# A hybrid encoder layer on one core: column weights stored as whole blocks of 128 columns

## The chip, the core and the metric

The kernel runs on one core of a Trainium2 chip. The metric is the time of one execution on the device, in microseconds. The kernel before takes 1960.93 us (median of 3 runs, 1960.2 to 1962.21). One more execution was taken with the hardware profiler on; it took 1962.87 us, of which 1961.1 us are the span between its first and its last instruction. All statements on waits and engines come from that execution.

The engines are TensorE (PE, matrix products; PEld is its loading of the stationary operand), VectorE (DVE), ScalarE (ACT), GpSimd (POOL) and SyncE (SP). In this kernel SP computes nothing; it issues transfers, and so does POOL. Transfers that SP issues are queue 1 of the profile, those that POOL issues are queue 0. The data of both are moved by the same 16 DMA engines.

## What is computed

The layer works on 1024 tokens of width 1024, in float32. With `rms` a root-mean-square norm with a learnt gain:

```python
h = x + 0.5 * (silu(n1 @ w_gate1) * (n1 @ w_up1)) @ w_down1       # n1 = rms(x), d_ff = 2816
z = rms(h) @ w_in                                                 # 1024 x 4352, cut into qA kA vA qB kB vB gA gB
yA = neighbourhood attention on a 16 x 64 grid, 8 heads, learnt relative bias
yB = banded attention, 8 query and 2 key/value heads, rope, one sink logit a head
h = h + (sigmoid(gA) * (yA @ w_a) + sigmoid(gB) * (yB @ w_b)) @ w_out
h = h + 0.5 * (silu(n2 @ w_gate2) * (n2 @ w_up2)) @ w_down2       # n2 = rms(h)
y = rms(h)
```

Seven of the weights stand on the left of a product in the kernel, so that it needs them a block of columns at a time: `w_gate` and `w_up` of both feed-forward parts (1024 x 2816 each), `w_in` (1024 x 4352) and the two branch weights `w_a` and `w_b` (512 x 1024 each). The change is to these seven. `w_down` and `w_out` are not touched.

## The kernel before

**Precision.** Each factor is split into a high part and a remainder (`split`, lines 86 to 89): ACT rounds the source to the short format (line 88), DVE, or POOL in a few places, subtracts that from the source (line 89). A product then takes three matmuls (`mm3`, lines 137 to 144): high by high (line 140), high by remainder (142), remainder by high (144). So before PE can start on a weight block, the block must have landed, ACT must have cast it and DVE must have subtracted.

**Fewer products.** The feed-forward parts, the larger part of the input projection and the output projection multiply 2 x 2 blocks with seven products in place of eight (`products`, line 241; its mirror for `w_down` and `w_out` is the class `Down`). For one step `i` and one of two matrices or column groups `m`, two blocks of 128 columns are loaded, each as 1024 rows by 128 columns: `raws[i, m, 0]` and `raws[i, m, 1]`. `prep(q)` (line 279) adds and subtracts quarters of them on DVE, splits the result, and `multiply(q)` (line 305) runs 4 x 3 matmuls of 128 x 512 on it. `prep` runs up to eight entries ahead of `multiply` (line 338 onwards). After every product `after` copies or adds the bank on ACT or DVE; the next product into the same bank waits for that.

**Loads of the seven weights.** Five places issue them, all on SP:

- `fetch` (line 277), called by `load` in `prep` for the raw blocks, and by `load_ahead` for the first entries of step 1;
- `load_ahead` (line 274), halves of blocks of step 2 (the first four of the eight groups of 128 rows for P1, the other four for P2);
- `load_split` (line 95), called by `load_w` for the blocks of `w_in` that make the gates gA and gB, which fill PE's time during attention (`gate`, line 890);
- `fetch_branch` (line 905), blocks of `w_a` and `w_b`, of 512 rows.

All take their source from `w_cols`:

```python
def w_cols(w, c0, n=P):
    return w[:, c0:c0 + n].rearrange("(c p) f -> p c f", p=P)
```

The weight lies in device memory row by row. A block of 128 columns is therefore 1024 pieces (512 for a branch weight) of 128 floats, 512 bytes, and partition p of the tile receives eight (four) of them: rows p, p + 128, p + 256 and so on.

**Buffers.** A raw tile is 128 x 1024 floats, 512 KB. There are four of them (tag `raw`), and `products` borrows two more from `fx` or `fa`. A new block can be requested only when the last reader of the old one is done, so SP waits in `fetch` for DVE.

**Stages in order of time.** First norm and transposes (0 to about 40 us); the first feed-forward part's gate and up (to about 430); its down projection (to about 610); a turn, in which the finished rows are normed, transposed and split while the first products of the next stage begin (`transition`, line 159; to about 690); the input projection (to about 860), with `rope` (line 701), which writes z to device memory, reads it back rotated and writes it again; attention with the gates as filler (to about 1146); branch products, merge and output projection (to about 1300); a second turn (to about 1380); the second feed-forward part (to the end).

**What sets the order.** The program text gives a priority; the framework's planner then writes out one fixed instruction list for each engine at build time, with its own estimates of how long each instruction and each transfer takes, and puts in the waits. On the chip each engine runs its list in order. In the profile of before one sees that the list isn't the order of the text: the casts for `T3` and `T4` (`strassen_rest`, line 225) stand on ACT ahead of the norm of the last row tile, which the text has earlier.

Of the kernel before, what the change touches and what calls it, by code (L numbers as in the profile page):

```python
# [15 lines left out]
P = 128  # L16
# [20 lines left out]
def trunk_kernel(ctx, tc, x, n1, wg1, wu1, wd1, nm, win, rpb, sink, wa, wb, wo,  # L37
# [12 lines left out]
    def nm_(s):  # L50
        uid[0] += 1
        return f"{s}_{uid[0]}"
# [25 lines left out]
    def raw4():  # L78
        return main.tile([P, 1024], F32, tag="raw", bufs=4, name=nm_("raw"))
# [4 lines left out]
    def ws4():  # L84
        return main.tile([P, 1024], F32R, tag="ws", bufs=8, name=nm_("ws"))

    def split(dst_hi, dst_lo, src, eng=None):
        nc.scalar.copy(dst_hi, src)  # L88
        (eng or nc.vector).tensor_tensor(dst_lo, src, f32v(dst_hi), op=ALU.subtract)  # L89

    def load_split(h, l, src_ap, a, b, r=None, eng=None):

        n = a * b
        r = raw4() if r is None else r
        nc.sync.dma_start(r[:, :n].rearrange("p (a b) -> p a b", a=a), src_ap)
        split(h[:, :n], l[:, :n], r[:, :n], eng)
        return (h[:, :n].rearrange("p (a b) -> p a b", a=a), l[:, :n].rearrange("p (a b) -> p a b", a=a))

    def w_cols(w, c0, n=P):
        return w[:, c0:c0 + n].rearrange("(c p) f -> p c f", p=P)  # L100

    def load_w(w, c0, r=None, eng=None):

        return load_split(ws4(), ws4(), w_cols(w, c0), w.shape[0] // P, P, r, eng)

    def load_gain(g):
        gb = const.tile([P, 1152], F32, tag="gain", bufs=1, name=nm_("gain"))
# [259 lines left out]
    def hidden(wg, wu, at_end):  # L367
# [4 lines left out]
        def after(i, p, m, bks, snap, sn):  # L372
# [37 lines left out]
            else:  # L410
# [14 lines left out]
                else:  # L425
# [5 lines left out]
                    put(i, "P6", s2)  # L431

        return products(lambda i, m, half: w_cols((wg, wu)[m], (i + half * NP) * P), NP, after, at_end, (6, 7),
                        [8, 9, 10, 11, 0, 1, 2, 3, 4, 5, 6, 7])

# [351 lines left out]
    def gate_first():  # L787
        mix["gate"] = load_w(win[0], GA + gates[0] * P, xs4())
# [10 lines left out]
    for c in range(4):  # L799
# [7 lines left out]
    hook(2, gate_first)  # L807
    hook(0, keep_u)
    pg = products(lambda i, m, half: w_cols(win[0], groups[i][m][half] * P), NG, store_z, at_end, (2, 3), range(8, 16),
                  ("P1", "P2", "P5", "P6", "P7", "P3", "P4"))  # L810
    down.into(transition(down1, gain, to_strassen, behind(pg), 2), pg)
# [144 lines left out]
    def filler():  # L956
        for dc, nxt in zip(gates, gates[1:] + [None]):
            if nxt is not None:
                yield from gate(dc, lambda: mix.update(gate=load_w(win[0], GA + nxt * P)))
            else:  # L960
                yield from gate(dc, lambda: [load_y(Y_B[c], c * P, nc.gpsimd) for c in range(2)])
        yield from branch_b()
        for i in range(2):
            branch_a(i)
            for _ in range(3):
                drain(a_mm[i][1], 1)
                yield
# [126 lines left out]
    for n in range(1 << 30):  # L1094
# [14 lines left out]
        if n in (59, 60, 61):  # L1109
            c = (59, 60, 61).index(n)  # L1110
# [53 lines left out]
    for i, dc in enumerate(a_order):  # L1164
        r = nxt.pop(0)
# [49 lines left out]
def _consts():  # L1215
# [14 lines left out]
    for cols in ((left, full, right), (full, full, full)):  # L1230
# [7 lines left out]
    return {"c_rope": rope, "c_mask_a": mask_a, "c_mask_b": mask_b}  # L1238


_INS = ['x', 'ffn1_norm', 'ffn1_w_gate', 'ffn1_w_up', 'ffn1_w_down', 'mix_norm', 'w_in', 'na_rpb', 'sink_logit',
        'w_branch_a', 'w_branch_b', 'w_out', 'ffn2_norm', 'ffn2_w_gate', 'ffn2_w_up', 'ffn2_w_down', 'final_norm']
_OUTS = [((1, 1024, 1024), 'float32')]
# [21 lines left out]
```

## Time and profile before

| | |
|---|---|
| median of 3 runs | 1960.93 us |
| profiled execution | 1962.87 us, span 1961.1 us |
| PE busy | 1927.7 us, 98% of the span |
| DVE / ACT / POOL busy | 1442.4 / 951.7 / 335.7 us |
| granted clock of PE, mean | 0.998 |
| bytes moved | 293.46 MB in 263554 packets |
| SP's queue | 206912 packets, 206.24 MB, 34.1% of the DMA engines' time |
| POOL's queue | 56512 packets, 85.58 MB, 15.3% |

The lines below are of these kinds. The page's first part gives an engine, its busy time and its instructions. The timeline gives start, duration (both us), engine, line of the code, operation, the tile written and the tiles read, shape, number, and in brackets the idle time of that engine just before it with what ended it. The view of stretches gives for a stretch of time the busy time of each engine with the number of instructions, PE's granted clock (1.00 is full), the busy share of the 16 DMA engines and the rate at which they moved data. On SP's timeline a row is the issue of a transfer, not its course.

### The profile page before, as it was taken

The numbers are of one execution on the slowest core, as the hardware profiler recorded it, in microseconds if no ns is written. First come the engines' busy times: TensorE is split into PE (matmuls) and PEld (weight loads), VectorE is DVE, ScalarE is ACT, GpSimd is POOL, SyncE is SP. The second block draws the span as 40 slices with busy tenths as digits, with TensorE's granted clock in tenths as the row PEclk, the third lists the DMA queues.
The fourth block names the chain that finished last, engine by engine and source line by source line (L and its number), as shares of the span: only waits on it lengthen the run. The fifth ranks groups of instructions, "written<-read, shape, count | busy, mean of one in ns | idle before, by whom it ended". The sixth has DMA issues, their size and how long they took to land. (4 is left out here: it accounts for less than half of the span.)

```text
span 1961.1 us, 25643 instructions
## 1 busy us (share of the span) xinstructions
PE 1927.7 (98%) x8968; PEld 1605.7 (82%) x8968; DVE 1442.4 (74%) x2543; ACT 951.7 (49%) x1845; POOL 335.7 (17%) x429
## 2 busy tenths in 40 slices
PE   7999999999999999999999999999999999999998
PEld 5888888888888878888888888887888888888886
DVE  7885566558967778678888857999766567559864
ACT  7433333334446543467787873366333333344452
POOL 1010011003400022311112135500101001005200
PEclk9999999999999999999999999999999999999999
DMA  6533323367243489953359565543433333493341
GB/s 195 172 119 123 102 92 120 110 221 268 85 125 122 136 206 241 227 177 92 101 137 195 179 223 209 178 145 98 150 108 113 108 97 102 142 347 107 116 137 60
DMA packets 263554, 293.46 MB, mean 150 GB/s; under 512 B 47072, under 2 KB 193888, under 8 KB 263424
## 3 DMA queue, kind: packets, MB, share of 16 engines
q1 hardware_dynamic: 206912, 206.24, 34.1%
q0 software_dynamic: 56512, 85.58, 15.3%
q8 instruction: 71, 1.16, 0.3%
q14 instruction: 59, 0.48, 0.1%
HBM read 205.16 MB, written 86.70 MB: 149 GB/s over the span
## 5 line engine op out<-in xcount | busy, mean ns | idle before, releaser
L140 PE MATMUL g<-ar,ws 128*128 128x512 f32 x1184 | 444.7, 397 | 8.0 <-ACT xs L901 1.9
L142 PE MATMUL g<-ar,ws 128*128 128x512 f32 x1184 | 437.5, 391 | 0.6 <-DVE ar L89 0.6
L144 PE MATMUL g<-ar,ws 128*128 128x512 f32 x1184 | 435.7, 390 | 1.5 <-DVE ws L89 1.5
L89 DVE TENSOR_TENSOR ws<-raw,ws 128x512 fp32r<-128x512 f32 (+1 forms) x329 | 239.4, 733 | 180.7 <-ACT ws L88 179.4
L88 ACT CAST ws<-raw 128x512 fp32r<-128x512 f32 (+1 forms) x331 | 209.1, 638 | 289.3 <-PE d L144 129.6
L144 PEld LDWEIGHTS g<-ar,ws 128*128 128x128 f32 x1184 | 222.7, 188 | 49.0 <-DVE ws L89 1.9
L140 PE MATMUL d<-ar,ws 128*128 128x512 f32 x680 | 262.3, 390 | 0.0
L142 PE MATMUL d<-ar,ws 128*128 128x512 f32 x680 | 261.9, 389 | 0.0
L144 PE MATMUL d<-ar,ws 128*128 128x512 f32 x680 | 261.9, 389 | 0.0
L142 PEld LDWEIGHTS g<-ar,ws 128*128 128x128 f32 x1184 | 223.0, 188 | 47.4 <-DVE ar L89 1.1
L140 PEld LDWEIGHTS g<-ar,ws 128*128 128x128 f32 x1184 | 217.5, 189 | 51.0 <-ACT ar L88 4.2
L140 PEld LDWEIGHTS d<-ar,ws 128*128 128x128 f32 x680 | 127.7, 188 | 26.5
L144 PEld LDWEIGHTS d<-ar,ws 128*128 128x128 f32 x680 | 127.6, 188 | 26.4
L142 PEld LDWEIGHTS d<-ar,ws 128*128 128x128 f32 x680 | 127.7, 188 | 26.3
L370 POOL DMA_DIRECT2D hid<-fx x96 | 51.8, 540 | 402.1 <-DVE fx L418 168.9
L89 DVE TENSOR_TENSOR ws<-ar,ws 128x512 fp32r<-128x512 f32 x114 | 108.1, 956 | 9.0 <-ACT ws L88 9.0
L88 ACT CAST ar<-raw 128x512 fp32r<-128x512 f32 (+1 forms) x83 | 56.0, 678 | 88.3 <-PE g L142 47.9
L89 DVE TENSOR_TENSOR ws<-fa,ws 128x512 fp32r<-128x512 f32 x76 | 52.5, 691 | 57.7 <-ACT ws L88 57.4
L140 PE MATMUL g<-ws,ws 128*128 128x512 f32 x232 | 91.0, 392 | 0.0
L142 PE MATMUL g<-ws,ws 128*128 128x512 f32 x232 | 90.4, 390 | 0.0
L144 PE MATMUL g<-ws,ws 128*128 128x512 f32 x232 | 90.3, 389 | 0.0
L1042 ACT ACTIVATE fa<-fa,nmx 128x385 f32<-128x385 f32 (+3 forms) x128 | 75.5, 591 | 26.2 <-DVE nmx L1039 25.5
(237 smaller groups left out, 3516.6 us busy)
## 6 DMA issues: line engine op xcount, KB each, us to landing
raw<-hid SPq DMA_DIRECT2D x70, 512.0 KB
hid<-fx POOLq DMA_DIRECT2D x96, 256.0 KB, 2.3
raw<-in_ffn_w_up_dram SPq DMA_DIRECT2D x32, 512.0 KB
ar<-in_ffn_w_down_dram SPq DMA_DIRECT2D x32, 512.0 KB
raw<-in_ffn_w_gate_dram SPq DMA_DIRECT2D x28, 512.0 KB
hid<-fa POOLq DMA_DIRECT2D x54, 256.0 KB, 2.3
raw<-in_w_in_dram SPq DMA_DIRECT2D x27, 512.0 KB
ar<-zs_d POOLq DMA_DIRECT2D x48, 256.0 KB, 5.0
```

The lines of the kernel that those rows point to most:

```text
L88: nc.scalar.copy(dst_hi, src)
L89: (eng or nc.vector).tensor_tensor(dst_lo, src, f32v(dst_hi), op=ALU.subtract)
L140: nc.tensor.matmul(b, lhs[0], r[0], start=first, stop=False, **kw)
L142: nc.tensor.matmul(b, lhs[0], r[1], start=False, stop=False, **kw)
L144: nc.tensor.matmul(b, lhs[1], r[0], start=False, stop=last, **kw)
L370: nc.gpsimd.dma_start(hid[PRODUCTS.index(p), i], src)
L1042: nc.scalar.activation(pr, pr, AF.Exp, scale=-1.0, bias=nmx[:, s:s + 1], accum_out=ssum[:, s:s + 1])
```

## The change

The host reorders each of the seven weights before the run: it cuts the matrix into blocks of 128 columns, and inside a block stores for each of the 128 partitions all the values that this partition will receive, one after the other. A block then is one stretch of 512 KB (256 KB for a branch weight), in which partition p's 4 KB (2 KB) are contiguous. `w_cols` picks a block by its number and gives it the old shape, (p, c, f). The tiles receive the same values in the same places. `load_w` takes the number of rows from the last dimension, since the first no longer holds it. The number of loads, their bytes, their destinations and their issuers stay.

```diff
-    def w_cols(w, c0, n=P):
-        return w[:, c0:c0 + n].rearrange("(c p) f -> p c f", p=P)
+    def w_cols(w, c0):
+        return w[c0 // P].rearrange("p (c f) -> p c f", f=P)
 
     def load_w(w, c0, r=None, eng=None):
 
-        return load_split(ws4(), ws4(), w_cols(w, c0), w.shape[0] // P, P, r, eng)
+        return load_split(ws4(), ws4(), w_cols(w, c0), w.shape[-1] // P, P, r, eng)
...
+def _blocks(w):
+
+    k, n = w.shape[1:]
+    return w.reshape(k // P, P, n // P, P).transpose(2, 1, 0, 3).reshape(1, n // P, P, k)
+
+
+_BLOCKED = ['ffn1_w_gate', 'ffn1_w_up', 'w_in', 'w_branch_a', 'w_branch_b', 'ffn2_w_gate', 'ffn2_w_up']
...
-    data = {name: inputs[name] for name in _INS}
+    data = {name: _blocks(inputs[name]) if name in _BLOCKED else inputs[name] for name in _INS}
```

The reordering is done on the host ahead of the launch and is not part of the time.

## The prediction

> **What bounds the kernel now.** I read the page's first part, then the stretches, then every idle time of PE.
>
> ```profile
> span 1961.1 us, 25643 instructions
> PE 1927.7 (98%) x8968; PEld 1605.7 (82%) x8968; DVE 1442.4 (74%) x2543; ACT 951.7 (49%) x1845; POOL 335.7 (17%) x429
> DMA packets 263554, 293.46 MB, mean 150 GB/s; under 512 B 47072, under 2 KB 193888, under 8 KB 263424
> q1 hardware_dynamic: 206912, 206.24, 34.1%
> ```
> ```profile
> 200.00:220.00 20.00, 20.00 (x90) 16.55 (x89) 15.87 (x25) 7.68 (x13) 2.16 (x4) 1.00 0.23 79
> 1340.00:1360.00 20.00, 20.00 (x90) 16.57 (x89) 19.80 (x34) 8.85 (x17) 0.54 (x1) 1.00 0.36 104
> ```
>
> PE is busy for 1927.7 of 1961.1 us. In a steady stretch (200 to 220) it starts some 89 matmuls in 20 us, 0.225 us each, at full clock, while the DMA engines are busy 0.23 of the time. A load that lands sooner there shortens nothing: SP waits for room and PE waits for nobody.
>
> ```profile
> SPq L277 <- DVE ws L89: 599.3, 89, 24.0
> ```
>
> In the list of SP's waits that is the largest: 599.3 us, in 89 waits, until DVE gives a raw buffer back. So the change can only act through the 33.4 us in which PE is idle, and only where the last thing that PE's chain waits for is one of the seven weights.
>
> The largest part of that idle time is the start, and there it isn't:
>
> ```profile
> 10.57 1.06 ACT L118 ACTIVATE xs<-fx 128x1024 f32<-128x1024 f32 x1 [0.16 <-DMA fx<-in_x_dram]
> 20.26 0.79 PE L140 MATMUL g<-ar,ws 128*128 128x512 f32 x1 [0.57 <-ACT ar L88]
> 29.78 0.50 PE L144 MATMUL g<-ar,ws 128*128 128x512 f32 x1 [1.48 <-DVE ws L89]
> 20.00:40.00 20.00, 17.80 (x81) 14.23 (x82) 19.22 (x31) 17.93 (x33) 1.96 (x3) 1.00 0.56 135
> ```
>
> The last wait of ACT for a transfer before 40 us ends at 10.57, for x, which was queued ahead of the weights and isn't changed. After that PE waits for ACT (20.26) and DVE (29.78), and these two are busy 17.93 and 19.22 of 20 us. I give the start nothing.
>
> **What the change removes.** From the code and the page's list of issues, 142 times 512 KB of weights are loaded (96 of gate and up, 38 of w_in, 8 of branch weights), 1024 pieces of 512 bytes each, 145408 in all. After it, 128 whole loads are 128 pieces of 4 KB, and 28 loads of 256 KB are 128 pieces of 2 KB: 16384 + 3584 = 19968. The page's packets should fall from 263554 to about 138100, queue 1 from 206912 to about 81500, at the same bytes. No instruction is added on any engine.
>
> **What a load gains.** Two prices, first the rate of the DMA engines when they are full, then a lone load from issue to use:
>
> ```profile
> 14.00:18.00 4.00, 2.52 (x11) 2.15 (x12) 3.56 (x7) 3.99 (x9) 0.92 (x1) 1.00 1.02 406
> 709.00:713.50 4.50, 4.50 (x21) 3.75 (x20) 3.68 (x6) 1.43 (x3) 0.00 (x0) 1.00 1.16 290
> ```
> ```profile
> 1209.07 0.34 SPq L1147 DMA_DIRECT2D raw<-g_d  x1
> 1212.33 1.06 ACT L1149 ACTIVATE raw<-raw 128x1024 f32<-128x1024 f32 x1 [1.09 <-DMA raw<-g_d]
> ...
> 1316.74 0.38 SPq L277 DMA_DIRECT2D ahead<-in_ffn_w_gate_dram  x1
> 1317.46 1.13 SPq L277 DMA_DIRECT2D ahead<-in_ffn_w_up_dram  x1
> 1321.54 0.62 ACT L88 CAST ws<-ahead 128x512 fp32r<-128x512 f32 x1 [1.28 <-DMA ahead<-in_ffn_w_gate_dram]
> 1323.65 1.14 ACT L88 CAST ws<-ahead 128x512 fp32r<-128x512 f32 x2 [0.97 <-DMA ahead<-in_ffn_w_up_dram]
> ```
>
> From 14 to 18 us the rows of x (4 KB) come at 406 GB/s; from 709 to 713.5 only w_in comes, at 290. For 512 KB that is 1.29 against 1.81 us: 0.52 us less at least. A lone 512 KB load of 4 KB rows (g_d) is in use 3.26 us after its issue; the weight loads at 1316.74 and 1317.46 take 4.80 and 6.19. So a lone load gains 1.5 us, a second one right behind it some 2.4 (6.19 less 3.26 less 0.5 for its place behind the first).
>
> [...]
>
> **The five places where a late weight load reaches PE.**
>
> ```profile
> 663.30 0.39 SPq L277 DMA_DIRECT2D ahead<-in_w_in_dram  x1
> 668.59 0.62 ACT L88 CAST ws<-ahead 128x512 fp32r<-128x512 f32 x1 [2.10 <-DMA ahead<-in_w_in_dram]
> 669.76 0.69 DVE L89 TENSOR_TENSOR ar<-fa,ar 128x512 fp32r<-128x512 f32 x1 [0.67 <-ACT ar L88]
> 671.25 0.69 DVE L89 TENSOR_TENSOR ar<-fa,ar 128x512 fp32r<-128x512 f32 x1 [0.20 <-ACT ar L88]
> 677.38 0.62 ACT L88 CAST ar<-fa 128x512 fp32r<-128x512 f32 x1 [1.00 <-DVE fa L208]
> 678.10 0.47 PE L140 MATMUL g<-ar,ws 128*128 128x512 f32 x1 [0.83 <-ACT ar L88]
> ```
>
> (1) The first turn. ACT stands 2.10 us for a weight; behind it stand its casts of the transposed rows, on these DVE's subtractions, on these the last norm, the cast at 677.38 and PE's 0.83. The load gains about 1.8 us here (5.3 us from issue to use against 3.5), but DVE has only 0.67 + 0.20 = 0.87 us of idle time for ACT in between to give back. PE gets 0.85. Bounds 0.5 (the rate alone) and 1.0.
>
> ```profile
> 709.75 0.69 DVE L295 TENSOR_TENSOR s<-fx 128x512 f32<-128x512 f32 x1 [3.20 <-DMA fx<-in_w_in_dram]
> 720.41 0.68 DVE L690 SCALAR_TENSOR_TENSOR fa<-g,fa 128x512 f32<-128x512 f32 x1
> 721.15 0.50 PE L140 MATMUL g<-ar,ws 128*128 128x512 f32 x1 [1.10 <-DVE fa L690]
> ...
> 724.14 0.68 DVE L690 SCALAR_TENSOR_TENSOR fa<-g,fa 128x512 f32<-128x512 f32 x1
> 724.88 0.50 PE L140 MATMUL g<-ar,ws 128*128 128x512 f32 x1 [0.68 <-DVE fa L690]
> ```
>
> (2) The input projection. DVE waits 3.20 us for the second of two blocks, then runs without a pause up to the eviction at 720.41, for which PE waits; the next wait of PE, at 724.88, comes through the same queue and the rope load of z, which is itself released by an earlier eviction of this chain. The two waits cost 1.10 and 0.68, and 0.16 more each until matmuls follow one another again: 2.1. Two blocks gain 1.04 us by the rates, at most the 3.20; nearest are two lone loads, of which part is spent beside POOL's writes. I take 1.5, all of which reaches PE. Bounds 1.0 and 2.1.
>
> ```profile
> 1142.34 0.62 ACT L88 CAST ws<-raw 128x512 fp32r<-128x512 f32 x1 [2.45 <-DMA raw<-in_w_branch_b_dram]
> 1143.94 0.63 PE L1069 MATMUL g<-ws,fx 128*128 128x256 f32 x4
> 1144.88 0.37 ACT L1007 COPY s<-g 64x256 f32<-64x256 f32 x1
> 1145.80 1.07 ACT L901 COPY xs<-g 128x512 f32<-128x512 f32 x2
> 1146.46 1.03 PE L140 MATMUL g<-ar,ws 128*128 128x512 f32 x2 [1.89 <-ACT xs L901]
> 1140.00:1160.00 20.00, 18.11 (x78) 14.83 (x77) 12.77 (x20) 13.15 (x19) 5.50 (x4) 0.91 0.87 256
> ```
>
> (3) The end of attention. ACT waits 2.45 us for a branch weight, and PE then 1.89 us for the copy at 1145.80. But the copy at 1144.88 stands before it in ACT's list and reads PE's last attention product, which ends at 1143.94 + 0.63: with the weight there in time, PE starts about 0.35 us earlier. Bounds: nothing, and 3.5 if the wait goes whole and with it the stretch of lower clock behind it (0.91 of 20 us, 1.8 us at most, of which I count 1.4).
>
> (4) The second turn, the two loads priced above. ACT loses 1.28 and 0.97 us, all of which the new loads give back. What follows:
>
> ```profile
> 1326.38 0.69 DVE L89 TENSOR_TENSOR ar<-fa,ar 128x512 fp32r<-128x512 f32 x1 [1.39 <-ACT ar L88]
> 1331.14 0.47 PE L140 MATMUL g<-ar,ws 128*128 128x512 f32 x1 [1.56 <-DVE fa L413]
> ```
>
> DVE waits 1.39 us for ACT and from there on is nearly without pause until PE's 1.56. PE gets 1.5. Bounds 1.0 (two loads, by the rate) and 1.7. Late next is DVE, which is full here (19.80 of 20 us in the stretch from 1340).
>
> ```profile
> 1367.99 0.69 DVE L295 TENSOR_TENSOR s<-raw 128x512 f32<-128x512 f32 x1 [1.94 <-DMA raw<-in_ffn_w_up_dram]
> 1376.55 0.50 PE L140 MATMUL g<-ar,ws 128*128 128x512 f32 x1 [0.38 <-DVE fx L413]
> ```
>
> (5) Behind it, DVE waits 1.94 us for a block of w_up and PE 0.38, with its restart 0.54. DVE gains more than that: 0.5, by either price of a load.
>
> **The sum.** 0.85 + 1.5 + 0.35 + 1.5 + 0.5 = 4.7 us; by the bounds 3.0 to 8.8. On the profiled execution, 1961.1 + 1.8 around it = 1962.87, that gives 1958.2. The median of the runs is 1.9 us below that execution, so on the scale of the medians 1960.93 - 4.7 = **1956.2 us**, by the bounds 1952.1 to 1957.9.
>
> **The rivals.**
>
> *A, the next chain is as late.* DVE takes the place of ACT in both turns. For it: DVE's 19.80 of 20 us; in (1) only 0.87 of ACT's 2.10 us can pass. Against it: DVE has named idle time in front of each chain. If (1) and (4) give a third and (2) only its rate: 0.3 + 0.7 + 0 + 0.5 + 0.2 = 1.7, so 1959.2 us.
>
> *B, slower by another order.* The planner writes each engine's list from its own estimate of when a load lands. If it takes the new loads for shorter, it puts casts and subtractions of weights ahead of evictions in the two turns, where ACT and DVE have no room. The price: the additions and splits for one P5 are five DVE instructions of 0.60 us, 3.0 us; from the point where an eviction is later than one product (12 matmuls x 0.225 = 2.7 us) PE stands. At one such step in each turn, 6 us: 1967 us. For it: the lists of before already differ from the text. Against it: bytes and priorities are the same, and how the planner prices short pieces the trace doesn't show. The same freedom could bring 6 us at the start, 1950.
>
> *C, the loads don't get faster.* The access keeps the shape (p, c, f); if the pieces aren't joined, all stays as it was, 1960.9. No load of before has this form, so the trace can't say. A second way to the same time is that 512-byte rows are at full rate already. [...]
>
> **How the numbers follow.** Forecast 0.48, A 0.25, B 0.15 slower and 0.05 faster, C 0.07 (0.04 by pieces that aren't joined, 0.03 by a rate that is full already). A run of this kernel tells 0.2%, 3.9 us, from no change. Of the forecast, some 0.4 lies below 1957.0 and 0.08 above. Faster: 0.4 + 0.05 = 0.45. Within: 0.08 + 0.25 + 0.07 = 0.40. Slower: 0.15. The forecast's own range is 1952 to 1958; to hold 8 in 10 with A, C and part of both sides of B it is 1950 to 1964.
>
> **What would show it.** Right: about 138100 packets; no wait of ACT or DVE for w_in, gate, up or branch_b longer than 0.5 us at the five places; no wait of PE over 0.6 us between 660 and 730 and between 1320 and 1380; the same 0.225 us a matmul in between. Wrong: A, if these waits of ACT go and PE's stay, now on DVE; B, if the instructions of ACT and DVE in the turns stand in another order and PE waits for evictions; C, if the packets stay at 263554. A gain before 40 us or inside the feed-forward parts would show that I misread what bounds them.

## The result

The changed kernel takes 1957.44 us (median of 12 runs, 1955.96 to 1959.79), the kernel before beside it 1961.82 us (12 runs). The ratio is 0.9978, with an interval of 0.9970 to 0.9986: 4.4 us less, about 0.2%. Two more series of the same kernel gave 0.9975 (0.9964 to 0.9985) and 0.9972 (0.9961 to 0.9983).

The profile after, first part and queue 1:

```profile
span 1957.3 us, 25643 instructions
PE 1926.9 (98%) x8968; PEld 1604.8 (82%) x8968; DVE 1439.6 (74%) x2543; ACT 951.4 (49%) x1845; POOL 336.6 (17%) x429
...
DMA packets 138114, 293.46 MB, mean 150 GB/s; under 512 B 47072, under 2 KB 48480, under 8 KB 137984
q1 hardware_dynamic: 81472, 206.24, 32.1%
```

The packets are those that were worked out, at the same bytes and with the same instructions. PE is nearly as busy as before (1926.9 against 1927.7 us), so of the 3.8 us by which the span of the profiled execution is shorter, 3.0 are idle time. In the steady stretches PE's part of the row is the same as before:

```profile
200.00:220.00 20.00, 20.00 (x90) 16.54 (x89) 16.08 (x25) 7.47 (x13) 2.28 (x5) 1.00 0.21 78
1340.00:1360.00 20.00, 20.00 (x90) 16.57 (x89) 19.78 (x34) 9.23 (x17) 1.08 (x2) 1.00 0.35 118
```

The lists of PE, DVE, ACT, POOL and SP hold the same instructions in the same order in both kernels (8968 matmuls, 2543 instructions on DVE, 1845 on ACT, 429 on POOL). So the k-th of the 8968 matmuls in one trace is the k-th in the other, and the time between two given matmuls can be compared directly. Over the long stretches between the places below, up to 312 us, the two traces agree to 0.03 us (0.12 in attention); the difference lies at a few places. Two places more move without a side: at the start of attention (862 to 872) this profile is 0.43 us slower than before, and the two other profiles of the same kernel are 0.33 and 0.22 faster; between 1235 and 1245 the three differ from before by +0.23, +0.17 and -0.04. The timeline after, at the first turn and the projection:

```profile
663.11 0.38 SPq L277 DMA_DIRECT2D ahead<-in_w_in_dram  x1
667.84 0.62 ACT L88 CAST ws<-ahead 128x512 fp32r<-128x512 f32 x1 [2.04 <-DMA ahead<-in_w_in_dram]
669.02 0.69 DVE L89 TENSOR_TENSOR ar<-fa,ar 128x512 fp32r<-128x512 f32 x1 [0.28 <-ACT ar L88]
670.50 0.69 DVE L89 TENSOR_TENSOR ar<-fa,ar 128x512 fp32r<-128x512 f32 x1 [0.19 <-ACT ar L88]
677.35 0.47 PE L140 MATMUL g<-ar,ws 128*128 128x512 f32 x1 [0.28 <-ACT ar L88]
...
700.68 0.93 SPq L277 DMA_DIRECT2D fx<-in_w_in_dram  x2
708.32 0.69 DVE L295 TENSOR_TENSOR s<-fx 128x512 f32<-128x512 f32 x1 [2.52 <-DMA fx<-in_w_in_dram]
719.72 0.50 PE L140 MATMUL g<-ar,ws 128*128 128x512 f32 x1 [0.40 <-DVE fa L690]
```

ACT and DVE still wait for these weights, 2.04 and 2.52 us where they waited 2.10 and 3.20. PE's waits fell from 0.83 to 0.28 and from 1.10 to 0.40. At the end of attention:

```profile
1140.00 0.62 ACT L88 CAST ws<-raw 128x512 fp32r<-128x512 f32 x1 [1.02 <-DMA raw<-in_w_branch_b_dram]
1142.54 0.37 ACT L1007 COPY s<-g 64x256 f32<-64x256 f32 x1
1143.03 0.63 PE L1069 MATMUL g<-ws,fx 128*128 128x256 f32 x4
1144.12 0.70 PE L140 MATMUL g<-ar,ws 128*128 128x512 f32 x2 [0.47 <-ACT xs L901]
...
1160.45 1.31 ACT L88 CAST ws<-raw 128x512 fp32r<-128x512 f32 x2 [1.97 <-DMA raw<-in_w_branch_b_dram]
1162.30 0.74 PE L140 MATMUL g<-ar,ws 128*128 128x512 f32 x2 [0.95 <-ACT ar L954]
```

ACT's wait fell from 2.45 to 1.02 us and PE's by as much, from 1.89 to 0.47. A part is given back further on: by a short wait of PE, 0.34 us up to 1147.89, and, in the last two rows, by a new one of 0.95 us, again behind a branch weight. At the second turn and behind it:

```profile
1314.96 0.33 SPq L277 DMA_DIRECT2D ahead<-in_ffn_w_gate_dram  x1
1315.63 1.12 SPq L277 DMA_DIRECT2D ahead<-in_ffn_w_up_dram  x1
1319.28 0.62 ACT L88 CAST ws<-ahead 128x512 fp32r<-128x512 f32 x1 [0.79 <-DMA ahead<-in_ffn_w_gate_dram]
1321.19 1.14 ACT L88 CAST ws<-ahead 128x512 fp32r<-128x512 f32 x2 [0.77 <-DMA ahead<-in_ffn_w_up_dram]
1328.69 0.47 PE L140 MATMUL g<-ar,ws 128*128 128x512 f32 x1 [0.87 <-DVE fa L413]
...
1360.01 0.33 SPq L277 DMA_DIRECT2D raw<-in_ffn_w_up_dram  x1
1365.07 0.69 DVE L295 TENSOR_TENSOR s<-raw 128x512 f32<-128x512 f32 x1 [1.48 <-DMA raw<-in_ffn_w_up_dram]
```

From issue to use the gate load takes 4.32 us where it took 4.80, the up load 5.56 (6.19), the w_up load 5.06 (1362.47 to 1367.99: 5.52): about 0.5 us less each (0.48, 0.63, 0.46), not 1.5 and 2.4. The total had come out as forecast with loads that gained a third of their price. That is what the runs had to explain.

### The profile page after: what moved, and what is told of

The parts are those of the page before. It is cut to its first block, busy times and chain, and to the rows that moved or that the text cites. A ratio compares the mean times of both kernels' runs of the same rounds, so it can differ in the third digit from the quotient of the medians.

```text
span 1957.3 us, 25643 instructions
## 1 busy us (share of the span) xinstructions
PE 1926.9 (98%) x8968; PEld 1604.8 (82%) x8968; DVE 1439.6 (74%) x2543; ACT 951.4 (49%) x1845; POOL 336.6 (17%) x429
## 2 busy tenths in 40 slices
DMA packets 138114, 293.46 MB, mean 150 GB/s; under 512 B 47072, under 2 KB 48480, under 8 KB 137984
## 3 DMA queue, kind: packets, MB, share of 16 engines
q1 hardware_dynamic: 81472, 206.24, 32.1%
## 4 chain that ended last, share of the span: by engine, by line
PE 87%; issue 5%; DVE 3%; DMA 2%; POOL 2%; ACT 2%; POOLq 0%; SPq 0%; DVEq 0%; ACTq 0%
PE g L140 16%; PE g L142 16%; PE g L144 16%; PE d L144 11%; PE d L140 11%; PE d L142 11%; PE d L1055 2%; PE g L1074 1%; PE d L1034 1%; PE g L1069 1%; PE d L1035 1%; DVE ar L89 1%; POOL zs_d L666 1%; DVE ws L89 1%; PE d L133 0%
```

## The experiments

Theory T: a load lands sooner because its pieces are longer, and this counts only at the named places. Its rivals: the DMA engines are less busy everywhere (S), or what helps is that a block lies in one stretch of memory (L).

### One part at a time

Each kernel keeps the host's block layout for some of the weights only, and `w_cols` reads the others as before:

```diff
     def w_cols(w, c0):
-        return w[c0 // P].rearrange("p (c f) -> p c f", f=P)
+        if len(w.shape) == 3:
+            return w[c0 // P].rearrange("p (c f) -> p c f", f=P)
+        return w[:, c0:c0 + P].rearrange("(c p) f -> p c f", p=P)
...
-_BLOCKED = ['ffn1_w_gate', 'ffn1_w_up', 'w_in', 'w_branch_a', 'w_branch_b', 'ffn2_w_gate', 'ffn2_w_up']
+_BLOCKED = ['ffn1_w_gate', 'ffn1_w_up', 'ffn2_w_gate', 'ffn2_w_up']
```

(for the other two `['w_in']` and `['w_branch_a', 'w_branch_b']`). What was expected:

> Only gate and up of both feed-forward parts are stored as blocks; w_in and the branch weights are read as before. Theory T (a load lands sooner because its pieces are longer, and that counts only where the profile of before shows a chain of PE waiting for it): the second turn (1.73 us of PE idle before to about 1.0), the wait for DVE at 1376 (0.54 to 0) and the wait at 1735 (0.74 to 0) shrink, the first turn, the projection and the end of attention stay: about -2.0 us against before. Rival S (the gain is spread over the steady stretches, because the DMA engines are less busy everywhere): by bytes, about two thirds of the 4.4 us, -3.0 or more, with the steady stretches shorter.

> Only w_in is stored as blocks. T: the first turn (0.99 us of PE idle to about 0.44) and the projection (2.09 to about 1.34) shrink, the rest stays: about -1.3 us, or up to 0.3 less where the wait behind the projection grows. S: by bytes about a quarter of 4.4, -1.2 us, but without a place.

> Only the two branch weights (8 loads of 256 KB, 1.4% of the bytes of the seven) are stored as blocks. T: the wait at the end of attention (2.06 us of PE and about 1.4 us of lower clock behind it) goes in part, about 0.6 us remain, and new waits behind it give part back: -1.0 to -2.3 us. S: less than 0.1 us.

Measured against before: gate and up 0.9998 (0.9990 to 1.0007), w_in 0.9995 (0.9986 to 1.0004), branch weights 0.9996 (0.9987 to 1.0005). None of the three can be told from no change by itself, and in the means they give only 0.2, 1.0 and 0.7 us; the 2.0 that T expected of gate and up lies at the edge of its interval, and the 0.7 of the branch weights is below T's 1.0 to 2.3, though the interval reaches them. The traces are clearer than the times. In each, the stall of the weights that were changed shrinks, and the others stay, as far as single profiles tell. With w_in alone PE has a new wait of 1.49 us at 1236.74; the second profile of that kernel doesn't have it, and it stays unexplained. With the branch weights alone the end of attention looks as in the changed kernel, the wait that gives a part back included:

```profile
1145.32 0.70 PE L142 MATMUL g<-ar,ws 128*128 128x512 f32 x2 [0.52 <-ACT xs L903]
...
1163.43 0.73 PE L142 MATMUL g<-ar,ws 128*128 128x512 f32 x2 [0.94 <-ACT ar L956]
```

while the projection keeps its waits (0.98 and 0.67 us). S falls: no steady stretch gets shorter in any of the three, and with the branch weights alone PE's wait at the end of attention falls by 1.37 us (1.89 to 0.52). The expectation counted these weights as 8 loads and 1.4% of the bytes of the seven, but the profile has 6144 packets fewer, 384 for each load of 256 KB: 16 loads, 5.6% of those bytes, by which S would give 0.25 us.

### Short pieces in whole blocks

```diff
     def w_cols(w, c0):
-        return w[c0 // P].rearrange("p (c f) -> p c f", f=P)
+        return w[c0 // P].rearrange("(c p) f -> p c f", p=P)
...
-    return w.reshape(k // P, P, n // P, P).transpose(2, 1, 0, 3).reshape(1, n // P, P, k)
+    return w.reshape(1, k, n // P, P).transpose(0, 2, 1, 3)
```

> All seven weights are stored as whole blocks of 512 KB (256 KB) at one stretch, but inside a block row by row, so that each partition still gets pieces of 512 bytes. T: 263554 packets as before, the waits of before, 0 us (within 1). Rival L (what helps is that a block lies in one stretch of device memory, not that its pieces are long): about -4 us at 263554 packets.

Measured: 1.0005 (0.9996 to 1.0013). The first part of its page, and two waits of PE:

```profile
DMA packets 263554, 293.46 MB, mean 150 GB/s; under 512 B 47072, under 2 KB 193888, under 8 KB 263424
...
722.33 0.50 PE L140 MATMUL g<-ar,ws 128*128 128x512 f32 x1 [2.13 <-DVE fa L690]
...
1147.52 0.71 PE L140 MATMUL g<-ar,ws 128*128 128x512 f32 x2 [1.61 <-ACT xs L901]
```

L falls as the cause of the gain: the block in one stretch brings nothing that the times show (1.0005); the length of the pieces does (0.9978 with long pieces in the same blocks). The two waits were 1.10 and 1.89 us before, so the first is longer here and the second a little shorter. A single profile says little at this size: the three profiles of the changed kernel itself, the same program, lie 1.2 us apart at the end of attention (24.79 to 26.00 us in the table below).

### The whole again, and the whole without the branch weights

The three parts add up to 1.9 us in the means, the whole had given 4.4. So the changed kernel was timed again, beside one with `_BLOCKED` less the two branch weights.

> The changed kernel itself, beside the runs of before on this chip, since the three parts alone gave -0.2, -1.0 and -0.7 us in the mean, -1.9 together, where the whole gave -4.4. Theory Add (each place gains by itself, the difference is scatter of chips and runs): between -2 and -3.5 us. Theory Joint (the parts help one another, since a stretch that ends sooner brings the next loads forward): -4.4 again. In the profile both expect the same places as in the first look: about 0.4 us of PE idle at the first turn, 1.3 at the projection, 0.6 at the end of attention with a new wait of about 1.1 us some 17 us behind it, and no wait at 1735.

> Gate, up and w_in are stored as blocks, the two branch weights are read as before. Add: what the whole gives here, less some 0.7 us that the branch weights gave alone. Joint: the whole less more than that (over 1.5 us). In the profile the wait at the end of attention stays (about 2 us of PE and a stretch of lower clock behind it) and the new wait 17 us behind it is absent.

Measured on one chip: the whole 0.9975, 5.2 us less in the means; without the branch weights 0.9982 (0.9974 to 0.9991), 3.4 us. The branch weights are worth 1.8 us here, gate, up and w_in together 3.4 us, where alone they had given 1.2. Scatter or a joint effect? So the two went beside the whole on a third chip:

> The changed kernel a third time, as the measure for the two parts that run beside it on the same chip. So far: -4.4 and -5.2 us in the mean against the runs of before on their chips. Both theories below expect -4 to -5 again.

> Gate and up alone as blocks, now beside the whole. All but the branch weights gave -3.4 us on another chip, gate and up alone -0.2 and w_in alone -1.0. Theory Add (the parts add, the first look had scatter or a chip of its own): gate and up gain only at the second turn and 1376, by the tables of the six profiles 0.6 + 0.6 us: -1.2, and with w_in alone and the branch weights (-0.7) it comes to the whole. Theory Joint (a place gains only when all its traffic is in long pieces): -0.2 again, w_in alone -1.0 again, and 2 to 3 us of the whole belong to no part.

> w_in alone as blocks, beside the whole. Add: first turn 0.5 to 0.6 us (in the first look of this kernel it was only 0.1), projection 1.1: -1.6 to -2.0. Joint: -1.0 again, with nothing at the first turn.

Measured: the whole 0.9972, gate and up 0.9992 (0.9983 to 1.0001), w_in 0.9987 (0.9978 to 0.9996). In the means 4.8, 1.7 and 2.0 us: 3.7 for the two, as the kernel without the branch weights had 3.4, and with 0.7 to 1.8 for the branch weights the sum holds the whole. That fits parts that add and a first series that was low by scatter. It is no more than a fit: each of these means is uncertain by some 1.8 us either way, over both series the two parts come to about 2.4 us, and a remainder of some 1 us that belongs to no part cannot be excluded. One place shows what may be a joint effect, by two profiles against four. The load of w_in at the first turn, with w_in alone in long pieces, and below it the same two rows of the whole (third series):

```profile
663.30 0.38 SPq L279 DMA_DIRECT2D ahead<-in_w_in_dram  x1
668.38 0.62 ACT L88 CAST ws<-ahead 128x512 fp32r<-128x512 f32 x1 [2.02 <-DMA ahead<-in_w_in_dram]
```
```profile
663.10 0.38 SPq L277 DMA_DIRECT2D ahead<-in_w_in_dram  x1
667.93 0.62 ACT L88 CAST ws<-ahead 128x512 fp32r<-128x512 f32 x1 [2.20 <-DMA ahead<-in_w_in_dram]
```

5.08 us from issue to use against 4.83. In five profiles with short w_in it was 5.3 to 5.5, in both with w_in alone 5.1 to 5.2, in four with gate and up long as well 4.7 to 4.8. SP's issues around this load (655 to 668 us) are of w_in, h and u, none of gate or up; why the layout of those matters here stays open.

### What each place is worth

Eleven profiles now share one order of instructions: before, the whole three times, and seven with other choices for the weights. For each place they were divided by whether its own weights were read in long pieces. The time is that between two fixed matmuls on either side of the place, in us:

| place (us of before) | short pieces, mean (range) | long pieces, mean (range) | gain | forecast [bounds] |
|---|---|---|---|---|
| 1, first turn (660 to 690) | 30.19 (30.07 to 30.31), 5 | 29.53 (29.42 to 29.62), 4 | 0.66 | 0.85 [0.5, 1.0] |
| 2, projection (690 to 735) | 45.23 (44.85 to 45.87), 5 | 43.96 (43.75 to 44.27), 6 | 1.26 | 1.5 [1.0, 2.1] |
| 3, end of attention (1143 to 1170) | 27.04 (25.23 to 27.61), 7 | 25.62 (24.79 to 26.00), 4 | 1.43 | 0.35 [0, 3.5] |
| 4, second turn (1315 to 1340) | 24.42 (23.98 to 24.99), 5 | 23.85 (23.50 to 24.33), 6 | 0.56 | 1.5 [1.0, 1.7] |
| 5, behind it (1375 to 1385) | 9.92 (9.55 to 10.12), 5 | 9.35 (9.29 to 9.52), 6 | 0.56 | 0.5 |
| a wait behind w_down (1700 to 1745) | 44.48 (43.97 to 45.13), 5 | 44.03 (43.97 to 44.18), 6 | 0.45 | none |

(The number of profiles stands behind the range. At the first turn the two with w_in alone, 29.86 and 29.98, are in neither group.) The gains add to 4.9 us; the three series gave 4.4, 5.2 and 4.8 in the means. The rows aren't equally firm. At places 1, 2 and 5 the two groups don't overlap; at places 3 and 4 they do. The last row is not sure: w_down is not changed, and two of the five profiles with short pieces are at the lower end as well.

Place 3 needs a word more. What differs without overlap there is PE's wait: 1.61 to 2.33 us in the seven profiles with short branch weights, 0.35 to 0.52 in the four with long ones. The time differs less cleanly, because six of the seven also have a stretch of lower clock behind the wait; the seventh, with short pieces in whole blocks, has not, and with 25.23 us it is quicker than three of the four with long pieces. The lower clock isn't met in every execution. The granted clock is on record for every run: one stretch of 3.41 us at half clock takes 0.0009 off its mean, and the end of the kernel, where PE is done and the clock is at half too, 0.0011 to 0.0018 in the profiles. So a mean of 0.999 leaves no room for a fall on the way, and one of 0.997 needs it. Of 86 runs of before, 33 show 0.999 (1960.6 us in the mean) and 16 show 0.997 (1962.2); 0.998 can be either. Of 27 runs of the changed kernel, 18 show 0.999 (1956.9) and none 0.997. Between runs without a fall the change thus gives 3.7 us, and the 1.43 of place 3, taken from profiles that nearly all had the fall, is likely more than a mean run of before loses there.

### What a lone load takes

The kernel's body is replaced: nothing is computed, tiles of 512 KB are loaded one at a time, and the next load may start when ACT has copied the last tile.

```python
for rep in range(2):
    for b in range(8):
        lone(f"short{rep}_", None, [plain(wg2[0], b)])      # 1024 pieces of 512 bytes
for rep in range(2):
    for b in range(8):
        lone(f"long{rep}_", None, [block(wg1[0], b)])       # 128 pieces of 4 KB
```

> Leaves out the whole computation: the kernel only loads tiles of 512 KB one at a time, the next when ACT has copied the last (0.9 to 1.1 us), eight of each kind: gate in pieces of 512 bytes, twice over; gate as blocks of 4 KB pieces, twice over; blocks written by the kernel itself shortly before; rows of x; then pairs of loads, short and long pieces. It measures issue to use with nothing else on the DMA engines. Theory Piece (as predicted: a lone load gains 1.5 us by long pieces; the small gain in the kernel comes from other traffic): 4.8 for short, 3.3 for long. Theory Rate (a load gains only the difference of the full rates): long 0.5 us less than short. If the memory is slower the first time a block is read (theory First): the second reading and the kernel's own blocks take about 1 us less than the first reading.

Its timeline (`scratch` are the blocks that the kernel itself wrote before):

```profile
10.19 1.04 ACT L63 COPY o<-short__3_71 128x1024 f32<-128x1024 f32 x1 [4.28 <-DMA short__3_71<-in_ffn_w_gate_dram]
...
74.56 0.37 SPq L61 DMA_DIRECT2D short__31_127<-in_ffn_w_gate_dram  x1
78.35 1.04 ACT L63 COPY o<-short__31_127 128x1024 f32<-128x1024 f32 x1 [3.82 <-DMA short__31_127<-in_ffn_w_gate_dram]
...
82.75 1.04 ACT L63 COPY o<-long__33_131 128x1024 f32<-128x1024 f32 x1 [3.35 <-DMA long__33_131<-in_ffn_w_gate_dram]
83.82 0.34 SPq L61 DMA_DIRECT2D long__35_135<-in_ffn_w_gate_dram  x1
87.25 1.04 ACT L63 COPY o<-long__35_135 128x1024 f32<-128x1024 f32 x1 [3.46 <-DMA long__35_135<-in_ffn_w_gate_dram]
...
148.19 1.04 ACT L63 COPY o<-long__63_191 128x1024 f32<-128x1024 f32 x1 [3.29 <-DMA long__63_191<-in_ffn_w_gate_dram]
...
218.69 1.04 ACT L63 COPY o<-scratch 128x1024 f32<-128x1024 f32 x1 [3.33 <-DMA scratch<-scr]
...
244.84 1.04 ACT L63 COPY o<-scratch 128x1024 f32<-128x1024 f32 x1 [3.28 <-DMA scratch<-scr]
```

In the rows a short load is in use 3.79 us after its issue, a long one 3.43; over the 16 loads of each kind it is 3.85 and 3.29 in the mean. Copy to copy it is (78.35 - 10.19) / 14 = 4.87 us for the short, (148.19 - 82.75) / 15 = 4.36 for the long, (244.84 - 218.69) / 6 = 4.36 for the kernel's own blocks. The long piece is worth 0.51 us, the 0.52 of the two rates. Theory Piece falls, and so does First: the second reading of the long blocks (4.37) takes what the first took (4.36), and own blocks are no faster.

This settles the price. The 3.26 us of g_d, from which 1.5 had come, are what a long load takes with the DMA engines to itself; the 4.80 of the gate load are some 1 us more than a short load takes alone. The change doesn't take that 1 us away: after it the same load takes 4.32, against 3.29 alone. What it is stays open. The only load beside it is that of up, issued 0.72 us behind it on the same queue; that this is the cause is argued and not tried alone, and the pairs below speak against a simple form of it.

Pairs of loads, from the same timeline, each row the first or the last of a series:

```profile
286.13 1.04 ACT L63 COPY o<-pshort__117_307 128x1024 f32<-128x1024 f32 x1 [2.73 <-DMA pshort__117_307<-in_ffn_w_up_dram]
...
318.03 1.04 ACT L63 COPY o<-pshort__143_359 128x1024 f32<-128x1024 f32 x1 [1.58 <-DMA pshort__143_359<-in_ffn_w_up_dram]
...
322.42 1.04 ACT L63 COPY o<-plong__147_367 128x1024 f32<-128x1024 f32 x1 [1.59 <-DMA plong__147_367<-in_ffn_w_up_dram]
...
359.48 1.04 ACT L63 COPY o<-plong__175_423 128x1024 f32<-128x1024 f32 x1 [1.73 <-DMA plong__175_423<-in_ffn_w_up_dram]
```

With two in flight a short load comes every (318.03 - 286.13) / 13 = 2.45 us, a long one every (359.48 - 322.42) / 14 = 2.65. In a second pass twelve long ones came every 2.2 us and the last four every 2.7. So beside another load the advantage can go. What switches between 2.2 and 2.7 wasn't tried. From issue to use a short load of a pair, once the series runs, takes some 3.85 us, as when it is alone; a long one 4.2 us in the first pass and 3.3 in the twelve of the second.

### Pieces of 256 bytes

A block is stored as 2048 pieces of 64 floats, and the accesses name them so:

```diff
-        return w[c0 // P].rearrange("p (c f) -> p c f", f=P)
+        return w[c0 // P].rearrange("(q p) f -> p q f", p=P)
...
-    return w.reshape(k // P, P, n // P, P).transpose(2, 1, 0, 3).reshape(1, n // P, P, k)
+    return w.reshape(k // P, P, n // P, 2, P // 2).transpose(2, 0, 3, 1, 4).reshape(1, n // P, 2 * k, P // 2)
```

> All seven weights as pieces of 256 bytes, 2048 for a load of 512 KB; 408962 packets by counting. Theory T (piece size sets how late a load lands, and only the named places count): by a straight line through 1.29 us for 128 pieces and 1.81 for 1024, a load takes 2.4 us at the full rate, 0.6 more than before; the first turn, the projection, the end of attention, the second turn and 1376 grow by 0.5 to 0.6 each (by twice that at the projection, with two loads): +3 to +4 us, while the steady stretches keep 0.225 us a matmul. If short pieces cost much more than the line, the steady stretches would starve as well: over +20 us. If piece size didn't matter: 0.

Measured: 0.9998 (0.9989 to 1.0006), where T had expected 3 to 4 us more. It is no test of T, because the lists are no longer the same: for this kernel the planner wrote another order (DVE's list differs at 249 of its 2543 places, ACT's at 118 of 1845, PE's at 53 of 8968). The page, and PE's longest new wait:

```profile
DMA packets 408962, 293.46 MB, mean 150 GB/s; under 512 B 337888, under 2 KB 339296, under 8 KB 408832
...
q1 hardware_dynamic: 352320, 206.24, 39.3%
...
1238.80 0.50 PE L143 MATMUL d<-ws,ws 128*128 128x512 f32 x1 [3.09 <-DVE raw L1182]
```

The pieces do cost: queue 1 holds 39.3% of the DMA engines' time where it held 34.1. Against before, the start loses 1.0 us, the first feed-forward part up to 612 us 0.8, the stretch from 800 to 880 3.0, that from 1235 to 1245 4.5; the two turns, the projection, attention and its end gain about as much in the other order. It shows that an order can move with the layout, as rival B had it: between 512 bytes and 4 KB the lists stay, at 256 bytes they don't. That the planner prices the pieces is likely but not shown, since the accesses have another shape here and `load_w` issues its load in a line of its own.

### Loads in halves

A load of 512 KB has 1.3 us of data, by the 406 GB/s from 14 to 18 us in before, and the first cast needs only the first half:

```diff
-                fetch(r, 1, m, 0)
+                for k in range(2):
+                    nc.sync.dma_start(r[:, 512 * k:512 * (k + 1)].rearrange("p (c f) -> p c f", f=P), src(1, m, 0)[:, 4 * k:4 * k + 4, :])
```

> The changed kernel, but the four loads of step 1 in each of the three places where the next stage's first blocks are loaded ahead are issued as two transfers of 256 KB (2 KB a partition) each, since the lone load of 512 KB takes 3.3 us of idle time of which some 0.65 is the second half's data, and the cast of the first half needs only the first. The planner writes another order for it. If the first half's earlier landing counts: 0.3 us less PE idle at the first turn and 0.4 at the second than with whole loads, -5 to -5.7 against before. If the extra issues on SP (0.4 us each) or the other order count for more: slower than the whole, -4 or less.

Measured: 0.9985 (0.9976 to 0.9994), beside the whole's 0.9972; in the means 2.7 us less than before against 4.8, with a wide scatter (1956.43 to 1962.77). The second turn, for which it was meant, is worse than with whole loads (0.87 in the first series):

```profile
1326.91 0.47 PE L140 MATMUL g<-ar,ws 128*128 128x512 f32 x1 [1.20 <-DVE fa L414]
```

The planner moved casts in all turns; whether the issues or the order cost it wasn't separated. No version here beats the changed kernel.

## Why the prediction was right, and where it was not

**The total.** Forecast 4.7 us, measured 4.4 (5.2 and 4.8 later). The mechanism held: the gain lies at the named places, the steady stretches and the start don't move, and the parts add within what the times can tell. S, L and rivals B and C fall: the lists stand in the same order, the packets are 138114, and the lone load is 0.51 us faster. Rival A had the second turn right (0.5 us in its sum), but not the projection and the end of attention. That the total came out so near is luck in part: its largest price was three times too high, the end of attention gave four times its term, and 0.45 us may lie at a place that wasn't in the sum.

**The price of a lone load** is the step that failed: "a lone load gains 1.5 us". It measured 0.51, the bound that the prediction had from the two rates (0.52). The two rows that it compared, 3.26 and 4.80 us, differed in more than their pieces: a load of either kind takes about 1 us longer at the second turn than alone (4.80 against 3.85 us, 4.32 against 3.29).

**Place 1**: 0.66 of 0.85, inside its bounds, but not by the limit that was given for it. The load was to gain 1.8 us, of which DVE's idle time of 0.87 let 0.85 through. It gained 0.56 (5.29 to 4.73 from issue to use), and DVE's two waits for ACT still stand at 0.28 and 0.19: the load's own gain was the limit, not DVE.

**Place 2**: 1.26 of 1.5. "All of which reaches PE" held: in the kernel before, DVE uses its second block 8.32 us after the issue of the pair (701.43 to 709.75), in the changed one 7.64 us (700.68 to 708.32), 0.7 us less, and PE's place is 0.75 shorter in the same two traces.

**Place 3**: 1.43 of 0.35, by a misread row. The copy at 1144.88 was taken to read PE's last attention product. After the change the copy in that position starts at 1142.54, ahead of the last product at 1143.03; it reads an earlier one. So nothing but the weight held ACT, and PE gets the whole of ACT's gain (2.45 to 1.02, 1.89 to 0.47). The stretch of lower clock went as well, as the upper bound had it. In this pair of traces the wait gives 1.43 us and the clock 1.60, and 1.92 are given back by the waits behind (0.34 about 1148, 0.95 at 1162.30; from start to start of the matmuls, until they follow at 0.227 us again, 0.66 and 1.26), which leaves 1.11. The wait at 1162.30 is 0.69 in the third series' profile, and there is none in the second's.

**Place 4**: 0.56 of 1.5, below the lower bound of 1.0. Two loads at half a microsecond each gave no more than one. And the profile of before was the worst of five here (24.99 us; the others 23.98 to 24.50).

**Place 5**: 0.56 of 0.5, as forecast.

**Of the signs named**, the packets and the 0.225 us a matmul came as said. ACT's and DVE's waits were to fall under 0.5 us; they stayed between 0.77 and 2.52. No wait of PE over 0.6 us was to be left in the turns and the projection; 0.62 us stayed at 723.36 and 0.87 at 1328.69. Both signs failed by the same price: the loads land sooner, but not soon enough to be there in time. The sum was right in part because the error at place 3 offset those at 1, 2 and 4.

## What to carry to other kernels

Here pieces of 4 KB in place of 512 bytes made a lone load of 512 KB 0.51 us faster, as the two rates had it (0.52), and that counted only where the last wait of the critical engine was that load; read those places, not the share of the queue. Compare a transfer's latency with one under the same conditions, at the same place or alone, before the difference is put down to one cause. And before a stall of 1 us is priced from one profile, look at the same stall in a second one, since some move by that much with nothing changed (PE's wait at 1162.30: 0.95 us, 0.69 and none in three profiles of one kernel).

## What the runs showed of the hardware

**The clock.** At the end of attention the granted clock fell to half for 3.41 us in six of the seven profiles with short branch weights, after pauses of PE of 1.89 us (before) to 2.33 us (w_in alone, second series). It did not fall in the seventh, with short pieces in blocks, after 1.61 us (1147.52, above), nor with long branch weights, after 0.35 to 0.52 us. The length of the pause alone doesn't tell: in the same seventh profile PE pauses 2.13 us up to 722.33 (above), and the clock stays at 1.00. Stretches of before with its pause of 1.89 us and the fall, and of the kernel with short pieces in blocks with both its pauses:

```profile
1143.23:1146.64 3.41, 1.52 (x9) 1.20 (x8) 1.73 (x5) 3.36 (x6) 2.65 (x2) 1.00 0.93 265
1146.64:1150.05 3.41, 3.41 (x9) 2.63 (x9) 3.36 (x4) 1.22 (x3) 2.55 (x2) 0.50 0.52 192
```
```profile
717.73:721.14 3.41, 2.46 (x11) 1.69 (x9) 3.38 (x7) 1.08 (x2) 1.00 (x2) 1.00 0.24 88
721.15:724.56 3.41, 2.23 (x10) 1.86 (x11) 2.89 (x5) 0.00 (x0) 0.54 (x1) 1.00 1.01 310
1144.40:1147.81 3.41, 1.80 (x10) 1.45 (x9) 1.73 (x5) 3.36 (x6) 2.76 (x2) 1.00 0.99 270
```

PE is busy for 1.52 us of the 3.41 ahead of the fall; in the three stretches of the other kernel it is busy for 2.46, 2.23 and 1.80 us, with the clock at 1.00. Why the clock falls after the one pause and not after the others was not shown. The fall costs 1.6 us: the 13 matmuls from the end of the pause take 4.64 us in before and 3.05 in the kernel with short pieces in blocks.

**Packets.** By queue 1's share of the 16 engines' time, 125440 packets fewer took it from 34.1 to 32.1% (31.0 and 31.5 in the other two profiles of the whole), 145408 more, of 256 bytes, to 39.3%. That is 2.0 to 3.1 points for the first number of packets and 5.2 for the second, in a kernel whose lists stand in another order.
